# Expert layer on one core: the output product over all 16384 expert rows, and over a list of used rows

## The chip, the cores and the metric

The kernel runs on one core of a Trainium2 chip. TensorE (PE) multiplies, VectorE (DVE) and ScalarE (ACT) work on SBUF and PSUM, GpSimd (POOL) works on SBUF and issues DMAs, SyncE (SP) only issues DMAs. PEld is TensorE's weight load. The metric is device time in microseconds, the median of several executions.

## The reference, cut to what matters

Two layers, 256 tokens of 1024 numbers, float32. Each layer ends in an expert mixer:

```
def peer_ffn(h, w_query, sub_keys, expert_u, expert_v):   # 256 tokens
    scores = (h @ w_query) . sub_keys          # 8 heads, 2 halves, 128 keys
    s_top, i_top = top_k(scores, 16)           # in both halves
    best, pos = top_k(all 16*16 sums, 16)      # 16 experts for each head
    expert_idx = i_top_half0 * 128 + i_top_half1   # of the chosen pairs
    gates = softmax(best)
    a = gelu(expert_u[expert_idx] . h) * gates     # 128 per token
    return sum over the 128 of a * expert_v[expert_idx]
```

There are 128 x 128 = 16384 experts, and a token uses 128 of them. The layer before the mixer is retention (layer 0) or a spatial gating unit (layer 1). The change touches neither.

## The kernel before, in words

The expert mixer is computed densely. An expert has the number i*128 + j. For each i there is a tile of 128 rows (the j's, on the partitions), and 128 such tiles in a layer.

- **Every weight tile** (128x1024 float32, 512 KB) comes in through `split_load`: SP loads `raw`, ACT rounds it to `hi` (L140), DVE forms the rest `lo` (L141). Products are three matmuls, hi by hi, hi by lo and lo by hi. `raw`, `hi` and `lo` have three buffers, and `weight` keeps two tiles ahead of the one in use.
- **First product**: `u_pair` multiplies two tiles of `peer_u` with the tokens and puts the gelu into A (tiles 0 to 71, kept in SBUF) or into `at`, which POOL writes to `a_dram` (the 56 tiles 72 to 127, L843).
- **Routing** (`route`, `gates`): top-16 on DVE, beside the first 36 pairs of the first product.
- **Gates**: during the last 28 pairs, `gather` builds for four tokens at a time one-hot matrices and multiplies them on PE (L820). The result is the gate of all 16384 experts for these tokens, nearly all of it zero. DVE multiplies tiles 0 to 71 of A with it in place (L824), ACT copies the other 56 to G (L826).
- **Output product**: for each of the 128 tiles, `gated` takes the product of A and G (from A, or reloaded from `a_dram`, L859, and multiplied on POOL, L871), ACT and DVE split it (L874, L875), and `out_proj` multiplies it with the tile of `peer_v`: two token blocks of 128, three matmuls, two halves of 512 columns, 12 matmuls of 512 columns in all (L347). The sums of all tiles stay in four PSUM banks. `adag` is woven in, one step for a pair: SP loads a tile of `ada_w`, DVE multiplies and adds it (L246). In layer 0 it has 32 such tiles, in layer 1 eight.

The program is written in the order in which the code runs. A planner keeps the order on each engine, by a simulated time line, and each engine takes its instructions in that order; a wait of the first holds those behind it. SP's and POOL's DMAs are such instructions too.

## Time and profile before

| | |
|---|---|
| median of 3 runs | 2140.42 us (2136.84 to 2141.46) |
| span of the profiled execution | 2136.0 us |
| DMA over the span | 455.50 MB, mean 213 GB/s |
| product of layer 0, layer 1 (first to last L347 of it) | 713 to 1060 us, 1775 to 2123 us |

The profiled execution's own time lies among the three runs, so 0.8 to 5.5 us above its span. Times in rows are microseconds from the start of the span, unless marked ns. A busy share is an average over stages with different limits, so the rows below are taken stage by stage.

### The profile page before, as it was taken

How to read it: one execution, taken by the hardware profiler on the slowest of the kernel's cores; microseconds unless marked ns; L12 is line 12 of the kernel's file. 1: busy time of each engine (PE TensorE's matmuls, PEld its weight loads, DVE VectorE, ACT ScalarE, POOL GpSimd, SP SyncE). 2: the span in 40 equal slices, each digit the busy share in tenths (PEclk: the TensorE clock that was granted, in tenths of full speed). 3: DMA queues.
4: the chain of work that ended last, by engine and by line, in shares of the span. 5: the costliest groups of instructions: out<-in, count | busy, mean ns of one | idle time of the engine just before them, and what ended most of it. 6: DMA issues, size and time to landing. Idle time of an engine off the chain costs nothing.

```text
span 2136.0 us, 35285 instructions
## 1 busy us (share of the span) xinstructions
PE 2067.6 (97%) x13440; PEld 1872.9 (88%) x13440; DVE 1642.5 (77%) x2908; ACT 1102.0 (52%) x1648; POOL 272.3 (13%) x286
## 2 busy tenths in 40 slices
PE   4999899999999999999999998999999999999998
PEld 4988799999999888888787787999999998888886
DVE  7877678998988677765677786789889886655565
ACT  2444444446777544444454534444467774444443
POOL 1000001100000100033202700011000001000332
PEclk8999999999999999999999999999999999999999
DMA  7678455555555788877656775555555557656774
GB/s 270 214 250 272 155 180 181 180 184 184 180 192 188 265 274 275 276 256 244 225 184 210 243 245 187 171 187 179 186 179 188 184 197 270 230 191 209 241 240 161
DMA packets 127497, 455.50 MB, mean 213 GB/s; under 512 B 15328, under 2 KB 17392, under 8 KB 126816
## 3 DMA queue, kind: packets, MB, share of 16 engines
q1 hardware_dynamic: 115056, 411.36, 57.7%
q0 software_dynamic: 11984, 39.79, 5.8%
q8 instruction: 105, 1.72, 0.3%
q10 hardware_dynamic: 288, 2.10, 0.3%
q14 instruction: 64, 0.52, 0.1%
HBM read 435.36 MB, written 17.83 MB: 212 GB/s over the span
## 4 chain that ended last, share of the span: by engine, by line
PE 92%; DVE 3%; DMA 1%; issue 1%; ACT 1%; POOL 1%; SPq 0%; DVEq 0%; ACTq 0%; POOLq 0%
PE acc L347 36%; PE ps L173 17%; PE ps L174 17%; PE ps L175 17%; PE gps L820 3%; DVE lo L141 1%; PE ps L667 1%; PE ps L292 1%; DMA x<-in_x 0%; PE ps L254 0%; DVE ada L246 0%; ACT hi L140 0%; POOL vr L591 0%; DMA raw<-in_sgu_out 0%; ACT ht L307 0%
## 5 line engine op out<-in xcount | busy, mean ns | idle before, releaser
L140 ACT CAST hi<-raw 128x1024 fp32r<-128x1024 f32 x680 | 713.6, 1050 | 788.1 <-PE ps L174 380.8
L141 DVE TENSOR_TENSOR lo<-raw,hi 128x1024 fp32r<-128x1024 f32 x680 | 855.7, 1259 | 290.4 <-ACT hi L140 288.3
L173 PE MATMUL ps<-hh,hi 128*128 128x256 f32 x2432 | 699.4, 288 | 7.1 <-ACT hh L312 7.1
L174 PE MATMUL ps<-hl,hi 128*128 128x256 f32 x2432 | 691.9, 285 | 0.8 <-DVE hl L313 0.7
L175 PE MATMUL ps<-hh,lo 128*128 128x256 f32 x2432 | 690.6, 284 | 1.1 <-DVE lo L141 1.1
L173 PEld LDWEIGHTS ps<-hh,hi 128*128 128x128 f32 x2432 | 468.7, 193 | 8.3 <-ACT hh L312 8.3
L174 PEld LDWEIGHTS ps<-hl,hi 128*128 128x128 f32 x2432 | 469.3, 193 | 1.4 <-DVE hl L313 1.4
L175 PEld LDWEIGHTS ps<-hh,lo 128*128 128x128 f32 x2432 | 468.5, 193 | 1.4 <-DVE lo L141 1.4
L347 PE MATMUL acc<-lo,wh 128*128 128x512 f32 x1008 | 311.6, 390 | 0.0
L347 PE MATMUL acc<-hi,wl 128*128 128x512 f32 x1008 | 310.5, 389 | 0.0
L347 PE MATMUL acc<-hi,wh 128*128 128x512 f32 x1008 | 271.5, 389 | 0.0
L347 PEld LDWEIGHTS acc<-hi,wl 128*128 128x128 f32 x1008 | 189.3, 188 | 39.4
L347 PEld LDWEIGHTS acc<-hi,wh 128*128 128x128 f32 x1008 | 189.1, 188 | 39.2
L347 PEld LDWEIGHTS acc<-lo,wh 128*128 128x128 f32 x1008 | 188.3, 188 | 38.4
L174 PE MATMUL ps<-lo,hh 128*128 128x512 f32 x320 | 126.3, 395 | 3.4 <-DVE lo L141 3.4
L175 PE MATMUL ps<-hi,hl 128*128 128x512 f32 x320 | 125.9, 394 | 0.0
L246 DVE SCALAR_TENSOR_TENSOR ada<-adaw,c_act,ada 128x1024 f32<-128x1024 f32 x84 | 107.7, 1283 | 19.2 <-PE acc L347 13.6
L711 POOL TENSOR_TENSOR eq<-eq,tif 128x512 f32<-128x512 f32 x32 | 56.6, 1785 | 454.4 <-DVE eq L706 405.9
L173 PE MATMUL ps<-hi,hh 128*128 128x512 f32 x320 | 112.8, 392 | 0.0
L871 POOL TENSOR_TENSOR at<-at,G 128x512 f32<-128x512 f32 x56 | 83.8, 1497 | 192.9 <-DMA at<-a_dram 192.8
L815 DVE TENSOR_TENSOR og<-oo,half 128x512 f16<-128x512 f16 x256 | 96.0, 417 | 0.1
L805 ACT ACTIVATE oo<-iota_f,jT 128x128 f16<-128x128 f32 x256 | 84.7, 431 | 5.3 <-PE gps L820 3.0
(215 smaller groups left out, 2000.2 us busy)
## 6 DMA issues: line engine op xcount, KB each, us to landing
raw<-in_peer_u SPq DMA_DIRECT2D x256, 512.0 KB, 3.5
raw<-in_peer_v SPq DMA_DIRECT2D x256, 512.0 KB, 4.3
adaw<-in_ada_w SPq DMA_DIRECT2D x96, 512.0 KB, 4.7
raw<-in_sgu_in SPq DMA_DIRECT2D x48, 512.0 KB, 4.4
raw<-in_ret_vg SPq DMA_DIRECT2D x32, 512.0 KB, 4.2
raw<-in_peer_q SPq DMA_DIRECT2D x32, 512.0 KB, 3.6
a_dram<-at POOLq DMA_DIRECT2D x56, 256.0 KB, 2.8
at<-a_dram POOLq DMA_DIRECT2D x56, 256.0 KB, 4.0
```

The source lines that it names most:

```text
L140: after_mark(nc.scalar.copy(hi, raw), after[0], ORDER)
L141: after_mark(nc.vector.tensor_tensor(lo, raw, f(hi), op=ALU.subtract), after[1], ORDER)
L173: first = nc.tensor.matmul(ps, ah, bh, start=start, stop=False)
L174: nc.tensor.matmul(ps, ah, bl, start=False, stop=False)
L175: marks["pe"] = nc.tensor.matmul(ps, al, bh, start=False, stop=stop)
L246: op = nc.vector.scalar_tensor_tensor(a, w, c_act[:, dc:dc + 1], a, op0=ALU.mult, op1=ALU.add)
L347: marks["pe"] = nc.tensor.matmul(accs[b][n], a[:, tb], bb[:, n * 512:(n + 1) * 512], start=first and a is lh and bb is wh, stop=False)
L711: nc.gpsimd.tensor_tensor(eq, eq, tif[:, :, a, :].unsqueeze(2).to_broadcast([P, NTB, TOPK, TOPK]), op=ALU.mult)
L805: nc.scalar.activation(oj[:, k // 2, :, k % 2], iota_f, AF.Abs, bias=jT[:, t0 + k:t0 + k + 1], scale=-1.0)
L815: nc.vector.tensor_tensor(og[:, q], oi[:, q].unsqueeze(1).to_broadcast([P, 2, P, 2]), gH[:, :, t:t + 2].unsqueeze(2).to_broadcast([P, 2, P ...
L820: nc.tensor.matmul(ps[:, 2 * q + k, :], oj[:, q, :, k], og[:, q, e, :, k], start=e == 0, stop=e == 1)
L871: nc.gpsimd.tensor_tensor(w, w, G[:, ip * 2 - n0:ip * 2 - n0 + 2, :], op=ALU.mult)
```

## The change

- A keeps only tiles 0 to 31 (`N0`). The first products of the other 96 (`NG`) are written by POOL to a table in DRAM, in two DMAs for a pair. The table has one line of 2 KB for each expert: activation and gate of token block 0, activation and gate of block 1, 128 tokens each.
- G is now one buffer for each token block. When a block is full, four times (24 tiles each) DVE takes the maximum over the 128 tokens (`flags`) and ACT issues a DMA that writes the gates to the table.
- `sort_rows` makes lists of used rows: those with a gate in block 0 alone, in both, and in block 1 alone. Room is for 23, 38 and 23 columns of 128 rows (`CAP`). Places come from prefix sums, the lists from one-hot products on PE (96 matmuls of 168 columns into one PSUM tile). A branch (`tc.If`) handles rows for which there is no room.
- The output product begins with 12 pairs (`FIRST`) of tiles 0 to 23 as before, while the lists are made (two steps for a pair, in the first ten). Then 19 units of two "both" columns, 23 units of one column of each "alone" list, and the four pairs left of A are interleaved. For each listed column POOL issues two indirect DMAs: 128 lines of the table (2 KB of a line, or 1 KB) and 128 rows of `peer_v` (4 KB each). An "alone" column has one token block, so 6 matmuls instead of 12.

```diff
-N0 = 72
+N0 = 32
+NR = 72
+NG = P - N0
-N1 = 128
+CAP = (23, 38, 23)
+NC = sum(CAP)
+FIRST = 12
 def split_load
+        if index is not None:
+            raw = listed["pool"].tile([P, 1024], F32, tag="vraw", bufs=5, name=nm("vraw"))
+            row_gather(raw, I["peer_v"], index)
+        else: ... nc.sync.dma_start(raw, src)
+    def row_gather(dst, table, index):
+        nc.gpsimd.indirect_dma_start(
+            out=dst, out_offset=None, in_=table,
+            in_offset=bass.IndirectOffsetOnAxis(ap=index, axis=0))
 def u_rows
+            for b in range(NTB):
+                nc.gpsimd.dma_start(cells[:, i1:i1 + 2, b, 0, :], tmp[:, :, b * P:(b + 1) * P])
 def gather
-                nc.scalar.copy(G[:, :, t0:t0 + 4], pi[:, n0:, :])
+            nc.scalar.copy(G[b][:, :, tt:tt + 4], pi[:, n0:, :])
+            if tt == P - 4:
+                for c in range(0, NG, 24):
+                    nc.vector.tensor_reduce(flags[:, b, c:c + 24], G[b][:, c:c + 24, :],
+                                            axis=AX.X, op=ALU.max)
+                    nc.scalar.dma_start(cells[:, 1 + c:25 + c, b, 1, :], G[b][:, c:c + 24, :])
 def lists
+            for i in range(0, NG, 8):
+                pm = pool.tile([P, 4, P, 2], F16, tag="pm", bufs=2, name=nm("pm"))
+                nc.vector.tensor_tensor(pm, iota_h..., pairs(ih[:, 0, i:i + 8], P), op=ALU.is_equal)
+                nc.vector.tensor_tensor(eq, cols_h..., pairs(ih[:, 1, i:i + 8], ncol), op=ALU.is_equal)
+                nc.vector.tensor_tensor(cm[:, :, 0], eq, pairs(rows_h[:, i:i + 8], ncol), op=ALU.mult)
+                nc.scalar.mul(cm[:, :, 1], eq, pidx)
+                for k in range(8):
+                    nc.tensor.matmul(ps, pm[:, k // 2, :, k % 2], cm[:, k // 2, :, :, k % 2], ...)
+                yield
 output product
+        def fetch(unit):
+            cell = vp.tile([P, 2, wide], F32, tag="cell" + kind, name=nm("cell"))   # 3 buffers
+            for a in range(2):
+                row_gather(cell[:, a], ag if kind == "b" else halves, listed["ag"][:, cs[a]:cs[a] + 1])
+        def gated(unit):
+            if kind == "b":
+                for b in range(NTB):
+                    nc.gpsimd.tensor_tensor(w[:, :, b * P:(b + 1) * P], cell..., cell..., op=ALU.mult)
+                return split_unit(w, T)
+            nc.gpsimd.tensor_tensor(w, cell[:, :, :P], cell[:, :, P:], op=ALU.mult)
+        for pos, unit in enumerate(order):
+            if pos < FIRST - 2: two steps of sorter
+            if last:
+                with tc.If(nc.values_load(listed["count"][:1, :1], min_val=0, max_val=NG * P) > 0):
+                    leftovers(*spare)
+            if pos + 2 < len(order):
+                fetch(order[pos + 2])
+            nxt = gated(order[pos + 1])
+            if kind == "x": half_proj(a, ...)      # 6 matmuls for a column
+            else: out_proj(accs, ...)              # 12 matmuls
```

## Rows read from the trace of the kernel before

**Rows 1.** Chain of waits in time order, the products: start, us, engine, tile, line, count.

```profile
713.01 60.33 PE acc L347 x266
...
949.78 110.66 PE acc L347 x488
...
1759.86 0.94 PE gps L820 x16
1775.23 60.32 PE acc L347 x266
...
1862.43 257.55 PE acc L347 x1136
```

**Rows 2.** Busy by stretch: us, engine busy (count), PEclk, DMA share, GB/s.

```profile
6.00:31.00 25.00, 6.10 (x40) 5.94 (x40) 21.00 (x33) 4.52 (x10) 2.13 (x2) 0.95 0.99 393
...
498.00:713.00 215.00, 215.00 (x2033) 212.59 (x2032) 182.26 (x368) 154.77 (x324) 19.68 (x31) 1.00 0.56 189
713.00:780.00 67.00, 67.00 (x302) 55.54 (x301) 48.05 (x50) 32.65 (x38) 5.36 (x5) 1.00 0.82 281
780.00:1060.00 280.00, 280.00 (x1252) 232.02 (x1251) 191.54 (x193) 134.20 (x154) 52.82 (x52) 1.00 0.79 260
...
1840.00:2123.00 283.00, 283.00 (x1254) 234.18 (x1253) 167.03 (x162) 135.21 (x155) 51.04 (x51) 1.00 0.65 212
```

**Rows 3.** Groups by line, DVE: name, shapes, count, busy us, mean ns, idle before.

```profile
L141 DVE TENSOR_TENSOR lo<-raw,hi 128x1024 fp32r<-128x1024 f32 x680 | 855.7, 1259 | 290.4 <-ACT hi L140 288.3
...
L246 DVE SCALAR_TENSOR_TENSOR ada<-adaw,c_act,ada 128x1024 f32<-128x1024 f32 x84 | 107.7, 1283 | 19.2 <-PE acc L347 13.6 <-PE ps L175 2.5 <-DMA adaw<-in_ada_w 2.4
L815 DVE TENSOR_TENSOR og<-oo,half 128x512 f16<-128x512 f16 x256 | 96.0, 417 | 0.1
...
L875 DVE TENSOR_TENSOR wl<-at,wh 128x512 fp32r<-128x512 f32 x56 | 40.4, 721 | 31.2 <-ACT wh L874 31.0
...
L715 DVE TENSOR_REDUCE sel<-eq 128x32 f32<-128x512 f32 x32 | 21.5, 671 | 2.6 <-POOL eq L711 2.4
...
L703 DVE CAST pf<-pa 128x64 f32<-128x64 uint32 x16 | 3.1, 194 | 0.5
```

**Rows 4.** Groups by line, POOL, costliest first.

```profile
L871 POOL TENSOR_TENSOR at<-at,G 128x512 f32<-128x512 f32 x56 | 83.8, 1497 | 192.9 <-DMA at<-a_dram 192.8
...
L859 POOL DMA_DIRECT2D at<-a_dram x56 | 32.4, 578 | 193.1 <-DVE wl L875 185.8 <-DMA a_dram<-at 7.3
L843 POOL DMA_DIRECT2D a_dram<-at x56 | 30.4, 543 | 386.8 <-ACT at L754 247.7 <-ACT G L826 129.8 <-ACT hi L140 9.3
```

**Rows 5.** Time line of POOL alone: one small read and multiply, start and us.

```profile
247.42 0.55 POOL L218 TENSOR_TENSOR rs<-v,mhalf 128x1 f32<-128x1 f32 x1 [1.30 <-DVE v L234]
```

**Rows 6.** Time line of DVE, gates and then tail of the first product.

```profile
600.60 0.75 DVE L815 TENSOR_TENSOR og<-oo,half 128x512 f16<-128x512 f16 x2
...
708.25 1.23 DVE L141 TENSOR_TENSOR lo<-raw,hi 128x1024 fp32r<-128x1024 f32 x1 [1.61 <-ACT hi L140]
711.12 1.23 DVE L141 TENSOR_TENSOR lo<-raw,hi 128x1024 fp32r<-128x1024 f32 x1 [1.65 <-ACT hi L140]
```

**Rows 7.** DMA issues: queue, count, KB each, median us from issue to landing.

```profile
raw<-in_peer_v SPq DMA_DIRECT2D x256, 512.0 KB, 4.3
...
a_dram<-at POOLq DMA_DIRECT2D x56, 256.0 KB, 2.8
at<-a_dram POOLq DMA_DIRECT2D x56, 256.0 KB, 4.0
```

**Rows 8.** Issue instructions of one line on SP: ns min/median/max.

```profile
L137 SPq DMA_DIRECT2D raw<-in_peer_v x256: 327/328/328, 700.2 to 2111.6; - x128
```

**Rows 9.** POOL's multiply L871 by itself: ns min/median/max.

```profile
L871 POOL TENSOR_TENSOR at<-at,G x56: 1273/1460/2324, 715.3 to 2105.7; 128x512 f32<-128x512 f32 x56
```

**Rows 10.** Time line of all engines, around one multiply on POOL.

```profile
726.00 1.22 DVE L141 TENSOR_TENSOR lo<-raw,hi 128x1024 fp32r<-128x1024 f32 x1
...
726.74 1.63 POOL L871 TENSOR_TENSOR at<-at,G 128x512 f32<-128x512 f32 x1 [3.88 <-DMA at<-a_dram]
...
727.76 1.69 DVE L141 TENSOR_TENSOR lo<-raw,hi 128x1024 fp32r<-128x1024 f32 x1 [0.55 <-ACT hi L140]
```

More of the change, by code (lines that the diff above doesn't have):

```diff
@@ L63, in peer_v_order, with unit_weights @@
 def peer_v_order():
-    n0, n1 = N0 // 2, N1 // 2
-    return list(range(n0)) + list(range(n0, n1)) + list(range(n1, P // 2))
+    nat = [("n", ip) for ip in range(N0 // 2)]
+    both = [("b", c) for c in range(CAP[1] // 2)]
+    one = [("x", c) for c in range(CAP[0])]
+    rest, last = nat[FIRST:], both.pop()
+    mixed = []
+    n = max(len(both), len(one))
+    for k in range(n):
+        for group in (both, one, rest):
+            mixed += group[len(group) * k // n:len(group) * (k + 1) // n]
+    return nat[:FIRST] + mixed + [last]
+def unit_weights(layer, kind, c):
+    if kind == "n":
+        return [("peer_v", layer, c * 2 + a) for a in range(2)]
+    if kind == "b":
+        return [("peer_g", layer, BASE[1] + c * 2 + a) for a in range(2)]
+    return [("peer_g", layer, BASE[0] + c), ("peer_g", layer, BASE[2] + c)]
 def weight_order():
@@ L94, in weight_order @@
             yield "peer_q", layer, m
-        for i in range(N1):
+        for i in range(P):
             yield "peer_u", layer, i
-        for ip in peer_v_order():
-            if ip * 2 >= N1:
-                for a in range(2):
-                    yield "peer_u", layer, ip * 2 + a
-            for a in range(2):
-                yield "peer_v", layer, ip * 2 + a
+        for unit in peer_v_order():
+            yield from unit_weights(layer, *unit)
 @with_exitstack
@@ L155, in weight @@
                 break
+            if k[0] == "peer_g":
+                ready.append((k, split_load(None, listed["v"][:, k[2]:k[2] + 1])))
+                continue
             src = I[k[0]]
-            for j in k[1:]:
-                src = src[j]
+            if k[0] == "peer_v":
+                src = src[bass.ds((k[1] * P + k[2]) * P, P)]
+            else:
+                for j in k[1:]:
+                    src = src[j]
             ready.append((k, split_load(src)))
@@ L765, in peer @@
         emitted = 0
-        slots = PH - 2 + n0 // 2
+        slots = PH - 2 + NR // 2
         q = None
-        for k in range(PH + n0 // 2):
+        for k in range(PH + NR // 2):
             marks["gate"] = marks["pe"]
@@ L773, in peer @@
             else:
[L774 to L775 removed]
+                u_rows(k - PH)
                 q = None
@@ new lines, in sort_rows @@
+        def sort_rows():
+            nc.vector.tensor_scalar(flags, flags, 0.0, None, op0=ALU.is_gt)
+            masks = lp.tile([P, 3, NG], F32, name=nm("masks"))
+            nc.vector.tensor_tensor(masks[:, 1], flags[:, 0], flags[:, 1], op=ALU.mult)
+            nc.vector.tensor_tensor(masks[:, 0], flags[:, 0], masks[:, 1], op=ALU.subtract)
+            nc.vector.tensor_tensor(masks[:, 2], flags[:, 1], masks[:, 1], op=ALU.subtract)
+            yield
+            place, left = numbers(masks, CAP, BASE, lp, ps_tile())
+            yield
+            for got in lists(place, NC, lp, ps_tile()):
+                yield
+            row, listed["v"] = got
+            agi = lp.tile([P, NC], I32, name=nm("agi"))
+            one, two, three = (slice(BASE[c], BASE[c] + CAP[c]) for c in range(3))
+            nc.vector.tensor_scalar(agi[:, one], row[:, one], 2.0, None, op0=ALU.mult)
+            nc.vector.tensor_copy(agi[:, two], row[:, two])
+            nc.vector.tensor_scalar(agi[:, three], row[:, three], 2.0, 1.0,
+                                    op0=ALU.mult, op1=ALU.add)
+            listed["ag"] = agi
+            yield
+            listed["left"] = left
+            count = lp.tile([P, 1], F32, name=nm("count"))
+            nc.vector.tensor_reduce(count, left, axis=AX.X, op=ALU.add)
+            ch = lp.tile([P, 1], F16, name=nm("ch"))
+            nc.vector.tensor_copy(ch, count)
+            ps = ps_tile()
+            nc.tensor.matmul(ps[:1, :2], ch, ones_h, start=True, stop=True)
+            ci = lp.tile([1, 2], I32, name=nm("ci"))
+            nc.vector.tensor_copy(ci, ps[:1, :2])
+            listed["count"] = ci
+            yield
@@ L880, in peer @@
+        sorter = sort_rows()
         nxt = gated(order[0])
-        for pos, ip in enumerate(order):
+        nstep = -(-18 // (FIRST - 2))
+        for pos, unit in enumerate(order):
             wh, wl = nxt
+            kind, c = unit
+            if pos < FIRST - 2:
+                for _ in range(nstep):
+                    next(sorter, None)
+            if pos == FIRST - 3:
+                drain(sorter)
+            last = pos == len(order) - 1
+            if last:
+                spare = ps_tile(), ps_tile()
+                with tc.If(nc.values_load(listed["count"][:1, :1], min_val=0, max_val=NG * P) > 0):
+                    leftovers(*spare)
```

210 lines of the change are left out of this document (168 added, 42 removed).

## The prediction

> **What bounds the kernel now.** I read the chain of waits first, in time order. In both products it is TensorE alone: layer 1 has one piece of 1136 matmuls in 257.55 us without a wait, 0.2267 us for one of 512 columns, and the pieces of layer 0 give the same [rows 1]. The table by stretch says the same: in the output product PE is busy all the time, DVE for 68% in layer 0 (191.54 of 280), POOL for 19%. In the last part of the first product (498 to 713) PE is also always busy, with DVE at 85% [rows 2]. So a matmul that goes is time that goes, as long as nothing else becomes the slowest. What could: DMA moves 260 GB/s there at a busy share of 0.79, while the start of the kernel, where loads alone set the pace, shows 393 GB/s at 0.99 [rows 2].
>
> **The change part by part, for one layer.**
>
> *Matmuls that go.* After the change there are 32 full tiles, 38 full columns and 46 half ones: 93 tiles' worth instead of 128. 35 x 12 x 0.2267 = **-95.2 us**. This holds only if the room suffices. I ran the reference's routing on its inputs: the lists hold 2599, 4753 and 2771 rows in layer 0, and 2665, 4383 and 2508 in layer 1, where 2944, 4864 and 2944 fit. So the branch is not taken.
>
> *Matmuls that come.* The lists take 96 of 168 columns. 16 gate matmuls of 128 columns take 0.94 us, 0.059 each [rows 1]; between that and 0.2267 for 512 columns, 168 columns come to 0.076: **+7.3** (5.7 to 21.8, by the two rows).
>
> *Used rows, block 0, amid the first product.* Four maxima of 3072 elements on DVE. One of 512 takes 0.671, and 512 more elements cost DVE 0.538 (1.259 for 1024 against 0.721 for 512, both split operations) [rows 3]: 3.36 each, 13.4 together, in one lump. DVE's 32.7 idle us of that stretch [rows 2] are spread, and a lump is covered only by the two tiles that are split ahead, 3.8 us each (215 us for 56 tiles): **+6** (0 to 13.4). ACT's four DMAs lie beside it if an issue is as short as SP's, 0.33 us [rows 8]. These have 3072 pieces of 512 bytes; if ACT were held until its 1.57 MB had gone, it would be 4.0 us each at 393 GB/s, 8.3 at 189, so 16 to 33 for a block. I take the short one, as the only HWDGE issue that the rows show; the long one stays in the range.
>
> *Used rows of block 1 and the lists, around the first ten pairs.* DVE has the second lump of 13.4. A list step compares and multiplies 1024 + 672 + 672 float16 numbers; two operations of 512 end 0.75 after the start, the second 0.335 later than the first (0.417 for one alone) [rows 3, 6], so 1.55 a step and 18.6 for twelve. About 38 small operations of at most 288 elements, at 0.25 each (0.194 for 64 elements [rows 3]), make 9.5. Together 41.5. Room: ten pairs last 54.4 us, and DVE is idle for 18.95 of 67 there [rows 2], 15.4; two further pairs 3.1; the last four tiles of the first product 1.6 each [rows 6], 6.5; two tiles ahead 5.4. 41.5 - 30.4 = **+11** (0 to 28). DVE's instructions are in order: behind the lists wait `lo` and `wl`, and for these PE.
>
> *POOL, the step that decides.* From the 13th unit on, each of 84 columns needs two indirect DMAs, and they sit in one queue with the multiplies. 168 issues; 61 multiplies of 256 elements (two for each of 19 units, one for each of 23) at half of 1.497 [rows 4], 0.75, make 45.8. The matmuls of this stretch (19 + 4 full units, 23 half) are 828 x 0.2267 = 187.7 us. No row shows an indirect DMA. From below, a direct one with 128 lines holds POOL for 0.54 to 0.58 [rows 4]. From above I take the multiply, which reads two whole operands on 128 partitions: 1.497 [rows 4]. An indirect one has to write as many descriptors and first to read one number from each partition, which is what the smallest POOL operation does, 0.55 [rows 5]. The two added give 1.1, my value; it lies in the middle of the bounds. Then POOL needs 168 x 1.1 + 45.8 = 230.6. It can begin about 10 us before PE gets there (two units in `vraw` and cells). 230.6 - 187.7 - 10 = **+33** (0 at 0.9 or less; +100 at 1.5). Landing is no limit: 4.0 us [rows 7], while a unit's four issues and its multiply last longer than that.
>
> *Transfers of that stretch.* 92 tiles of `peer_v` 48.2 MB, cells 16.0 MB, and in layer 0 23 tiles of `ada_w`, 12.1 MB: 76.3 and 64.2. Dividing rate by busy share gives 329 and 326 GB/s full in the two products, 397 at the start [rows 2]. So layer 0 needs 192 to 232 us and layer 1 162 to 197. Layer 1 is hidden behind POOL's 221. In layer 0 I take 228: **+7**, in layer 0 only.
>
> *The branch.* Every engine reads a count and jumps before the last unit. Nothing in the trace shows one. The bounds are 0 and three landings of 4.3 in a row [rows 7], 12.9 (the count, the code, the start again); I take **+5**, near one landing. None of these costs goes below nothing, since PE was never idle.
>
> *Costs nothing.* 96 writes of activations by POOL instead of 28 (0.54 each [rows 4]) are hidden by POOL's idle time: 19.7 busy of 215 [rows 2]. Reloads and multiplies of 28 pairs leave POOL; nobody waited for them, as PE shows no gap.
>
> **Sum.** Layer 1: -95.2 + 7.3 + 6 + 11 + 33 + 5 = -32.9. Layer 0: -25.9. Together -58.8. The profiled execution: 2136.0 - 58.8 = 2077 of span, and with the 4.4 by which the median of the runs stands above this span (its own time lies 0.8 to 5.5 above) **2082 us**.
>
> **A rule weighed.** POOL's multiply takes 1.273 at least, 1.497 on average and 2.324 at most [rows 4, 9], and a split on DVE that overlaps one takes 1.69 instead of 1.22 [rows 10]. The Trainium skill, "SBUF — State Buffer", section "Who interferes with whom", says that a DVE instruction with two SBUF inputs and a GpSimd instruction that reads SBUF hold each other off, the second waiting for the whole of the first. The trace agrees for the multiply. Whether it goes for the reading of an index list no row shows. By the rule it would, and by the multiply's mean delay (1.497 - 1.273 = 0.22) an issue would be 1.32, POOL +37 more in each layer, layer 0's transfers hidden behind it, and the sum 2149.
>
> **The rivals.**
>
> *A. An indirect issue costs as little as a direct one.* At 0.58 POOL needs 143 us and hides. PE sets the pace in layer 1; in layer 0 the transfers, 192 us at the best rate seen, +5. For: 128 descriptors in both. Against: the index list. Sum: -95.2 + 29.3 = -65.9 and -60.9, time **2014**. The Trainium skill, "DMA: Bandwidth & Descriptors", section "Specifications", gives about 358 GB/s as HBM's limit for a core; by it layer 0 would lose 20 us more. The 393 GB/s of rows 2 are above that.
>
> *B. Slower: POOL's queue holds PE up for longer than the matmuls saved.* The costs other than POOL's are 29.3 (layer 1), so the change loses once POOL costs 66, and that is 168 x t + 45.8 - 197.7 = 66: from **t = 1.29 us** for an issue. For: the queue is in order, so a wait for a free `vraw` or a cell adds to t; +0.22, as the multiply has it on average over its least [rows 4, 9], is enough; 128 numbers from as many partitions may be read one by one. Against: the bare sum of its two parts is 1.1. At 1.5 POOL costs 100, so +34 in each layer, the transfers of layer 0 being hidden: **2209**. ACT held by the gates' DMAs would add to this, but does not decide it.
>
> *C. Transfers decide, not POOL.* At 326 to 329 GB/s, +35 in layer 0 and 0 in layer 1 (197 against 197.7): with POOL at 0.9, **2043**. For: 4 KB rows in any order, and cells of 1 and 2 KB. Against: 397 at the start.
>
> *D. It doesn't do what it says.* If room ran out, the branch's 96 columns of 12 matmuls would add at least 261 us. The counts speak against it.
>
> **How the numbers follow.** Forecast (issue 1.0 to 1.25) 0.40, A 0.24, B 0.26, C 0.08, D 0.02. An issue of 0.1 us more is 34 us in all (less in layer 0 while the transfers hide it), so the forecast's own range is 2045 to 2130. The range has to reach well into A and B: **1995 to 2190**, which leaves out A at its luckiest (no lump, no branch cost) and B beyond t = 1.44. No change within 0.2% (4.3 us, about what a measurement of this kernel can tell) is the narrow strip about t = 1.29: 0.04, taken from the top of the forecast and the bottom of B. Faster 0.71, slower 0.25.
>
> **What would show it.** Groups by line: the mean of the indirect DMA on POOL, 1.1; under 0.9 is A, over 1.29 is B. By stretch: after the 12th pair, POOL busy over 95% and PE about 85%, with a stretch of some 220 us instead of 283 for the same tiles; if it is the DMA share that is at 0.95 or more and POOL has gaps, it is C. DVE without a gap from 700 to 770, and PE waiting for `lo` there for some 11 us. A gap in PE of 6 us where the first block of gates ends; a longer one with ACT idle means that ACT was held by its DMAs. What makes the prediction wrong is above all the issue time, and then anything that stops POOL's queue.

## The result, and the profile after

The changed kernel takes **2285.78 us** (median of 4 runs, 2283.4 to 2286.64) where the kernel before, run beside it, takes 2139.3: 1.0685 of it, interval 1.067 to 1.07. Forecast were 2082 us, range 1995 to 2190. The change makes the kernel 146 us slower; the sign was wrong, and the time lies beyond the range. The span is 2284.1 us, 148.1 more than before.

The head of the page (busy time, share, instructions; then the granted clock in 40 slices):

```profile
PE 2006.8 (88%) x12796; PEld 1757.7 (77%) x12796; DVE 1683.7 (74%) x3041; ACT 1091.9 (48%) x1636; POOL 791.5 (35%) x771
...
PEclk8999999999999988888999999999998989888998
```

The same line of the kernel before:

```profile
PE 2067.6 (97%) x13440; PEld 1872.9 (88%) x13440; DVE 1642.5 (77%) x2908; ACT 1102.0 (52%) x1648; POOL 272.3 (13%) x286
```

PE is busy 60.8 us less than before and yet the span grew: it now waits where it did not. The table by stretch of layer 0 shows where; the columns are those of [rows 2] (stretch, length, busy time of PE, PEld, DVE, ACT and POOL, then granted clock, DMA share, GB/s), whose second to fourth rows cover the same work.

```profile
498.00:611.50 113.50, 113.50 (x1068) 112.25 (x1067) 93.10 (x203) 87.33 (x176) 28.50 (x36) 1.00 0.64 197
611.50:636.00 24.50, 10.37 (x86) 9.69 (x85) 20.72 (x20) 7.01 (x13) 2.89 (x4) 0.72 0.99 281
636.00:712.00 76.00, 76.00 (x721) 75.05 (x720) 61.22 (x143) 58.65 (x123) 14.45 (x20) 0.98 0.64 198
712.00:746.50 34.50, 23.10 (x185) 22.12 (x183) 24.79 (x26) 8.72 (x13) 4.33 (x6) 0.85 0.94 282
746.50:821.00 74.50, 74.38 (x391) 59.70 (x390) 67.54 (x113) 40.26 (x47) 7.69 (x9) 1.00 0.80 264
821.00:839.00 18.00, 0.40 (x2) 0.00 (x0) 3.48 (x4) 2.40 (x3) 14.33 (x15) 0.57 0.75 254
839.00:1128.50 289.50, 231.58 (x835) 167.25 (x836) 173.40 (x172) 112.19 (x136) 242.28 (x211) 0.89 0.74 245
```

Three places lose. Behind each block of gates PE stands (rows two and four: 25.5 us idle, and the clock falls to 0.72 and 0.85). In front of the first half column it stands 18 us (row six). In the stretch of the listed columns (last row) it is busy for 80%, at a granted clock of 0.89, and POOL is the full engine, not PE: busy for 242 of 289.5 us, and nearly all the rest is the short gaps of the next rows.

POOL's groups (columns as in [rows 4]):

```profile
L168 POOL DMA_INDIRECT vraw<-in_peer_v,vi x168 | 201.1, 1197 | 110.8 <-DVE agi L1004 69.2 <-issue 32.9 <-DMA vraw<-in_peer_v,vi 3.0
L168 POOL DMA_INDIRECT cell<-ag_dram,agi x168 | 197.1, 1173 | 48.5 <-issue 41.1 <-DMA vraw<-in_peer_v,vi 3.4 <-POOL at L1062 1.9
...
L1057 POOL TENSOR_TENSOR at<-cell 128x256 f32<-128x256 f32 x76 | 74.7, 1008 | 0.6
...
L1062 POOL TENSOR_TENSOR at<-cell 128x256 f32<-128x256 f32 x46 | 49.6, 1079 | 0.7
```

An indirect DMA holds POOL for 1.185 us on average. Beside that the idle column shows 74.0 us of "issue" in the two groups: 0.30 us stand ahead of nearly each one. From POOL's first gather (812.9) to the end of its last (1121.5) its time line has no gap over 0.31 us: the queue is 308.6 us of work and these gaps, and 306.5 in layer 1. The time line of POOL where the queue starts shows both (start, us, and in brackets the idle time):

```profile
834.46 0.95 POOL L168 DMA_INDIRECT cell<-ag_dram,agi  x1 [0.30 <-issue]
835.72 0.94 POOL L168 DMA_INDIRECT vraw<-in_peer_v,vi  x1 [0.30 <-issue]
836.96 0.94 POOL L168 DMA_INDIRECT vraw<-in_peer_v,vi  x1 [0.30 <-issue]
837.92 0.74 POOL L1062 TENSOR_TENSOR at<-cell 128x256 f32<-128x256 f32 x1
```

The gap stands ahead of an indirect DMA and not ahead of a multiply, which starts 0.02 after the one before it. And the first multiply stands behind nineteen gathers, though the first cells were issued at 815.8 and land 4.6 us after their issue at the median; PE waits for that multiply and ACT's split of it, by its own time line:

```profile
839.15 1.22 PE L1069 MATMUL acc<-hi,wh 128*128 128x512 f32 x2 [17.75 <-ACT wh L1045]
```

**The account of both layers**, from PE's time line (ends of its pieces). A layer's output product ends with its last pair of tiles, whose 24 matmuls stand on other lines than the rest; 1060 and 2123 us, in the table of the kernel before, leave them out. The last matmuls of both layers, before and then changed:

```profile
1065.47 0.39 PE L175 MATMUL acc<-hi,wl 128*128 128x512 f32 x1
2125.03 0.39 PE L175 MATMUL acc<-hi,wl 128*128 128x512 f32 x1
```

```profile
1137.20 0.39 PE L209 MATMUL acc<-hi,wl 128*128 128x512 f32 x1
2272.80 0.39 PE L209 MATMUL acc<-hi,wl 128*128 128x512 f32 x1
```

Layer 0: first product +33.7 (746.7 against 713.0), first twelve pairs +9.4 (74.7 against 24 x 12 x 0.2267 = 65.3), gap +17.8, stretch from the first half column to the end 298.4 against 287.6 for the same tiles, +10.8: in all +71.7. Layer 1, from the end of layer 0's output product: +34.6, +8.6, +20.0 and +12.8 (297.7 against 284.9), in all +76.0. What follows it is 0.4 longer. The sum is the 148.1.

### The profile page after: what moved, and what is told of

The parts are those of the page before. It is cut to its first block, busy times and chain, and to the rows that moved or that the text cites. A ratio compares the mean times of both kernels' runs of the same rounds, so it can differ in the third digit from the quotient of the medians.

```text
span 2284.1 us, 34636 instructions
## 1 busy us (share of the span) xinstructions
PE 2006.8 (88%) x12796; PEld 1757.7 (77%) x12796; DVE 1683.7 (74%) x3041; ACT 1091.9 (48%) x1636; POOL 791.5 (35%) x771
## 5 line engine op out<-in xcount | busy, mean ns | idle before, releaser
L162 ACT CAST hi<-raw 128x1024 fp32r<-128x1024 f32 x488 | 509.7, 1048 | 582.1 <-PE ps L208 349.9
L163 DVE TENSOR_TENSOR lo<-raw,hi 128x1024 fp32r<-128x1024 f32 x488 | 616.1, 1266 | 126.6 <-ACT hi L162 120.7
L163 DVE TENSOR_TENSOR lo<-vraw,hi 128x1024 fp32r<-128x1024 f32 x168 | 222.1, 1327 | 231.9 <-ACT hi L162 225.7
L817 POOL DMA_DIRECT2D ag_dram<-at x192 | 139.0, 726 | 527.9 <-ACT at L807 519.2
L162 ACT CAST hi<-vraw 128x1024 fp32r<-128x1024 f32 x168 | 175.4, 1047 | 278.8 <-DMA vraw<-in_peer_v,vi 235.3
L168 POOL DMA_INDIRECT vraw<-in_peer_v,vi x168 | 201.1, 1197 | 110.8 <-DVE agi L1004 69.2
L168 POOL DMA_INDIRECT cell<-ag_dram,agi x168 | 197.1, 1173 | 48.5 <-issue 41.1
L397 PE MATMUL acc<-lo,wh 128*128 128x512 f32 x544 | 183.0, 419 | 2.5 <-DVE lo L163 1.5
L397 PE MATMUL acc<-hi,wl 128*128 128x512 f32 x544 | 175.4, 405 | 0.0
L397 PEld LDWEIGHTS acc<-lo,wh 128*128 128x128 f32 x544 | 106.0, 201 | 34.8 <-DVE lo L163 13.4
```

The lines of the kernel that those rows point to most:

```text
L162: after_mark(nc.scalar.copy(hi, raw), after[0], ORDER)
L163: after_mark(nc.vector.tensor_tensor(lo, raw, f(hi), op=ALU.subtract), after[1], ORDER)
L168: nc.gpsimd.indirect_dma_start(out=dst, out_offset=None, in_=table, in_offset=bass.IndirectOffsetOnAxis(ap=index, axis=0))
L397: marks["pe"] = nc.tensor.matmul(accs[b][n], a[:, tb], bb[:, n * 512:(n + 1) * 512], start=first and a is lh and bb is wh, stop=False)
L817: nc.gpsimd.dma_start(cells[:, i1:i1 + 2, b, 0, :], tmp[:, :, b * P:(b + 1) * P])
```

## The experiments

The stretch and the end of the first product are read from PE's time line in each kernel. For layer 1 the first product is counted from the end of layer 0's output product. The kernels e2, e3 and e4 fetch other rows than the listed ones; e5, e13 and e15 leave the gates out of the listed tiles, e6 and e15 miss used rows, and e8 leaves a rest out; the sizes and the number of matmuls stay.

| kernel | first product ends, layer 0 | first product, layer 1 | stretch, layer 0 / 1 | us | ratio to before |
|---|---|---|---|---|---|
| before | 713.0 | 709.4 | 287.6 / 284.9 for the same tiles | 2139.3 | 1 |
| changed | 746.7 | 744.0 | 298.4 / 297.7 | 2285.78 | 1.067 to 1.07 |
| e2_v_direct | 744.9 | 744.5 | 223.4 / 197.7 | 2085.7 | 0.970 to 0.980 |
| e3_cells_direct | 747.9 | 744.3 | 222.7 / 202.0 | 2093.92 | 0.974 to 0.984 |
| e4_both_direct | 747.9 | 740.8 | 217.1 / 189.4 | 2073.74 | 0.966 to 0.974 |
| e8_no_lo | 746.9 | 744.8 | 262.9 / 254.5 | 2205.18 | 1.028 to 1.034 |
| e7_in_order | 746.0 | 743.7 | 321.3 / 318.0 | 2299.6 | 1.072 to 1.078 |
| e1_gates_by_pool | 739.4 | 740.6 | 306.5 / 293.4 | 2293.93 | 1.065 to 1.080 |
| e5_long_pieces | 736.4 | 729.4 | 301.9 / 293.8 | 2255.61 | 1.051 to 1.058 |
| e6_short_maxima | 751.6 | 747.6 | 299.9 / 292.5 | 2272.94 | 1.060 to 1.066 |
| e9_spread | 754.0 | 745.8 | 299.5 / 294.2 | 2298.81 | 1.073 to 1.077 |
| e13_no_gate_writes | 736.2 | 734.1 | 303.6 / 293.0 | 2264.09 | 1.056 to 1.060 |
| e15_no_writes_short | 716.2 | 712.4 | 304.7 / 296.1 | 2222.87 | 1.034 to 1.041 |
| e10_80_listed | 740.7 | 738.7 | 269.6 / 258.8 | 2184.87 | 1.019 to 1.023 |
| e11_80_listed_dve | 742.3 | 735.8 | 255.8 / 234.3 | 2133.7 | 0.995 to 0.999 |
| e12_72_listed_dve | 739.0 | 731.7 | 267.0 / 248.4 | 2148.37 | 1.003 to 1.006 |
| e14_80_listed_paced | 735.9 | 724.5 | 239.5 / 218.0 | 2128.77 | 0.994 to 0.998 |

The theory after the result was that POOL's queue alone sets the end of the output product, and that the hold in the first product is ACT standing behind its own gate DMAs. The rivals were transfers, DVE, and the order of POOL's queue.

### Is it POOL's queue? Indirect DMAs replaced by direct ones

**e2_v_direct**: SP loads tiles of `peer_v` in order in place of the listed rows.

```diff
-            row_gather(raw, I["peer_v"], index)
+            nc.sync.dma_start(raw, I["peer_v"][bass.ds(tile * P, P)])
...
```

> The 84 listed columns of a layer take a contiguous tile of peer_v by SP's direct load (the wrong rows, the same bytes) into the same five buffers; the cells are still gathered. Theory (POOL's queue sets the pace: 168 issues of 1.48 us with the gap behind them, and multiplies of 62 us, 311 in all): 84 issues remain, POOL needs about 186 us, the stretch from the first half column falls from 289 to 195 to 215 us, and the time to 2070 to 2130. Rival (transfers set the pace: the bytes are the same): the stretch stays above 270 us, time above 2240. Rival (the planner's order on POOL, multiplies late behind gathers, sets it): the 18 us gap before the first half column stays and the time is 2180 to 2240.

**e3_cells_direct**: the cells instead, from lines of the table in order.

```diff
-                row_gather(cell[:, a], ag if kind == "b" else halves,
-                           listed["ag"][:, cs[a]:cs[a] + 1])
+                nc.sync.dma_start(cell[:, a], ag[bass.ds((1 + cs[a]) * P, P), :wide])
```

> The cells of the 84 listed columns come by SP's direct load from contiguous lines of the table (the wrong lines, the same bytes); peer_v's rows are still gathered by POOL. Theory (issues on POOL count, whatever they fetch): the same 84 issues fewer, so within 30 us of the run in which the rows of peer_v come direct, 2070 to 2130. Rival (rows of 4 KB in any order are what is slow, or the wait for cells): the time differs from that run by more than 60 us.

**e4_both_direct**: both edits.

> Both the cells and the rows of peer_v of the listed columns come by SP's direct loads (wrong rows, same bytes); POOL only multiplies. Theory (POOL's queue): POOL has 62 us of work and drops out; what is left is PE's 188 us or the transfers, 76 MB in layer 0 in 192 to 232 us; stretch 190 to 235 in layer 0 and 188 to 200 in layer 1, time 2050 to 2110. If the transfers were the bound all along, nothing is gained here either: above 2240.

Either half of the indirect DMAs taken away, with the same bytes and the same matmuls, turns the change into a gain: 2085.7 and 2093.92. 84 indirect DMAs fewer in a layer shorten the stretch by 75 to 100 us; 84 x 1.485 (1.185 and the 0.30 ahead) would be 125. The 84 that are left take longer, 1.317 and 1.346 on average, and PE is busy for 92% of layer 0's stretch in both, so that its own work is nearly the limit. Without any, layer 1's stretch is 189.4, PE's own 187.7; layer 0's is 217.1, and there the transfers are full, as this stretch of it shows:

```profile
839.00:1020.00 181.00, 167.41 (x719) 131.22 (x718) 160.02 (x155) 97.08 (x119) 68.90 (x54) 0.99 0.98 359
```

The DMA engines are full at 359 GB/s, and 217.1 is inside the prediction's 192 to 232 us for that traffic. DVE is busy for 160 of the 181 us too, and PE's waits name its `lo` for 11.0 of 15.3 us, so that the transfers alone hold layer 0 is argued, not shown. The Trainium skill, "DMA: Bandwidth & Descriptors", section "Specifications", names about 358 GB/s as HBM's limit for a core; this row agrees, the 393 of [rows 2] does not. The theory stands. The whole saving of the matmuls exists in layer 1 (284.9 to 189.4 for the same tiles) and 70 us of it in layer 0, and POOL's queue takes it and more.

### What makes an indirect DMA 1.19 us? The index read beside DVE

In layer 0, 54 of the 168 indirect DMAs have no DVE instruction beside them for over 0.3 us; their mean is 0.952. The 114 others have 1.32 (worked out from the time lines of POOL and DVE, 805 to 1125). **e8_no_lo** takes the larger of the two-input DVE instructions of the listed columns away (the correction term uses `hi` a second time; `wl` stays).

```diff
-        lo = spool.tile([P, 1024], F32R, tag="lo", name=nm("lo"))
+        lo = hi if index is not None else spool.tile([P, 1024], F32R, tag="lo", name=nm("lo"))
         after_mark(nc.scalar.copy(hi, raw), after[0], ORDER)
+        if index is not None:
+            return hi, lo
```

> For listed columns DVE doesn't form lo; the products take hi in its place (one split left out, matmuls the same). Theory (an indirect DMA waits on POOL for DVE operations with two SBUF operands: 1.32 us where they overlap, 0.96 where not): the mean issue falls from 1.185 to 1.0 to 1.08, multiplies from 1.0 to about 0.8, POOL saves 30 to 45 us a layer, time 2195 to 2235. Rival (contention is not what makes the long ones): the mean stays above 1.15 and the time above 2265.

2205.18, inside the theory's numbers. POOL's groups in it:

```profile
L170 POOL DMA_INDIRECT cell<-ag_dram,agi x168 | 171.8, 1023 | 49.7 <-issue 44.4 <-DMA cell<-ag_dram,agi 2.1 <-DMA vraw<-in_peer_v,vi 1.8
L170 POOL DMA_INDIRECT vraw<-in_peer_v,vi x168 | 167.6, 998 | 105.9 <-DVE agi L1006 65.6 <-issue 29.0 <-ACT hi L162 4.1
...
L1059 POOL TENSOR_TENSOR at<-cell 128x256 f32<-128x256 f32 x76 | 61.2, 831 | 0.8 <-DVE wl L1048 0.2
...
L1064 POOL TENSOR_TENSOR at<-cell 128x256 f32<-128x256 f32 x46 | 37.0, 804 | 0.8
```

No instruction of POOL was touched, and each became shorter: 1.185 to 1.01, the multiplies 1.03 to 0.82. The gap of 0.30 stayed. So DVE's operations with two SBUF inputs lengthen an indirect DMA as they lengthen a multiply. That it is the two inputs, and not DVE's being busy, the time lines of all runs bear out, in a few cases: 41 indirect DMAs that had only DVE's `adas` or `dg` beside them, with one such input at most, took 0.96 on average, 1068 with no DVE instruction beside them 0.95, and those beside one with two inputs 1.28 (six beside a wider instruction with one input, `ada<-adaw,c_act`, took 1.08). This is the rule that the prediction weighed and did not take (the Trainium skill, "SBUF — State Buffer", "Who interferes with whom"); it does go for the indirect DMA here.

### Does POOL's order matter?

**e7_in_order** ties POOL's gathers and multiplies into the order in which they are written, so that no multiply stands behind later gathers.

```diff
+    def in_order(inst):
+        after_mark(inst, listed.get("last"), ORDER)
+        listed["last"] = inst
+        return inst
...
-            row_gather(raw, I["peer_v"], index)
+            in_order(row_gather(raw, I["peer_v"], index))
...
```

> POOL's gathers and multiplies in the output product are kept in the order in which the program writes them, instead of the planner's, which puts 20 gathers ahead of the first multiply. Theory (POOL's total sets the end): the 18 us gap before the first half column shrinks, but the stretch behind it grows by as much; time 2270 to 2295. Rival (the order costs time by itself): 30 to 40 us less, 2240 to 2260.

The gap in front of the first half column falls from 17.8 to 4.2 us, the stretch grows from 298.4 to 321.3, and the whole gets 14 us slower, 5 us above the theory's numbers; the rival is out. Removing the gap wins nothing, since POOL's queue comes out no shorter: 318.4 us instead of 308.6 in layer 0. In order, POOL's multiplies also wait for their cells (9.7 us there).

### The first product: who holds PE?

The waits of PE in the changed kernel up to 760 name ACT alone (us in total, times, longest):

```profile
PE ps L207 <- ACT hi L162: 23.9, 3, 10.7
PE acc L397 <- ACT hi L162: 1.6, 1, 1.6
```

and ACT's time line shows it at its own DMA issues (`ACTq` is its queue):

```profile
611.51 16.62 ACTq L893 DMA_DIRECT2D ag_dram<-G x4
628.26 0.60 ACT L807 ACTIVATE at<-ps 128x512 f32<-128x512 f32 x1 [16.25 <-issue]
```

while DVE has its four maxima in the same stretch:

```profile
612.90 13.12 DVE L891 TENSOR_REDUCE flags<-G 128x24 f32<-128x3072 f32 x4
```

**e1_gates_by_pool** lets POOL issue the gate DMAs.

```diff
-                    nc.scalar.dma_start(cells[:, 1 + c:25 + c, b, 1, :], G[b][:, c:c + 24, :])
+                    nc.gpsimd.dma_start(cells[:, 1 + c:25 + c, b, 1, :], G[b][:, c:c + 24, :])
```

> Only change to the changed kernel: the sixteen DMAs that write the gates to the table are issued by POOL instead of ACT. Theory (ACT is held by its own DMA issue, 4 of them 16.6 us, twice a layer): ACT's wait in front of the gelu, 62.7 us in all, goes; PE's waits for hi at the two blocks (10.7 and 9.8 in layer 0) shrink to a few us that DVE's four maxima leave; time about 2225 us (2210 to 2240). Rival 1 (DVE's lump of 13.4 us makes the stall): ACT is free, but PE now waits for lo as long as before, time 2270 to 2286. Rival 2 (the table writes fill the DMA engines, share 0.99 there, and the weight tiles come late): PE waits for hi behind a late raw, time 2265 to 2286.

A miss: POOL issues each in 1.42 us, ACT is no longer held by an issue, and the first product ends only 7.3 us earlier; the first twelve pairs then lose 11.5. The time is 2293.93, no gain. PE's waits up to 760 already name DVE:

```profile
PE ps L209 <- DVE lo L163: 7.1, 2, 6.0
PE gps L882 <- DVE og L877: 5.9, 1, 5.9
```

**e5_long_pieces** writes the same gate bytes in runs of 12 KB to a buffer of their own (the table's gate half takes a second copy of the activations, so the product uses these in place of the gates).

```diff
-                nc.gpsimd.dma_start(cells[:, i1:i1 + 2, b, 0, :], tmp[:, :, b * P:(b + 1) * P])
+                for g in range(2):
+                    nc.gpsimd.dma_start(cells[:, i1:i1 + 2, b, g, :], tmp[:, :, b * P:(b + 1) * P])
...
-                    nc.scalar.dma_start(cells[:, 1 + c:25 + c, b, 1, :], G[b][:, c:c + 24, :])
+                    nc.scalar.dma_start(g_dram[layer][:, b, c:c + 24, :], G[b][:, c:c + 24, :])
```

> The gates of a block go, still in four DMAs on ACT with the same bytes, to a buffer of their own in pieces of 12 KB instead of 512 bytes; the table's gates take a second copy of the activations, written pair by pair (so gates are left out of the result). Theory (3072 short pieces hold ACT and crowd the DMA engines): the issue falls from 16.6 us for four to under 2, the first product ends 12 to 25 us earlier in layer 0 and stays ahead, time 2225 to 2265. Rival (DVE's lump of 13.4 us alone makes the stall at each block): the first product ends within 5 us of before, time 2275 to 2295.

In the stretch of the lump the DMA engines move 373 GB/s instead of 281 at the same share, and PE is idle 8.1 of 24.5 us instead of 14.1:

```profile
611.50:636.00 24.50, 16.44 (x126) 15.55 (x125) 22.48 (x26) 7.87 (x15) 5.78 (x8) 0.79 0.98 373
```

Four issues take 3.0 us instead of 16.62. So pieces of 512 bytes matter; but two thirds of the first product's loss in layer 0 stayed (23.4 of 33.7). The time came as the theory had it, the first product's gain in layer 0 did not (10.3, and 12 at least was expected).

**e6_short_maxima** lets DVE's maxima run over 8 of 128 tokens.

```diff
-                    nc.vector.tensor_reduce(flags[:, b, c:c + 24], G[b][:, c:c + 24, :],
+                    nc.vector.tensor_reduce(flags[:, b, c:c + 24], G[b][:, c:c + 24, :8],
```

> The maxima look at 8 of the 128 tokens of a block only (lists miss rows; every list, gather and product keeps its size). DVE's lump falls from 13.4 us to about 1.4. Theory (writes are the cause, the lump is hidden beside them): the first product ends within 8 us of the changed kernel's 746.7, and the time is 2262 to 2290, a little less by what the lump costs ahead of the lists. Rival (the lump is the cause): it ends 20 us earlier or more, time under 2250.

The first product ends later (751.6), not earlier. I read this as acquitting DVE, and that was wrong: e1's waits name it, and two later runs show it.

**e9_spread** cuts each block's writes and maxima into twelve, one a step.

```diff
-                for c in range(0, NG, 24):
...
+                pending.extend((b, c) for c in range(0, NG, 8))
...
             step[0] += 1
+            spill_gates(1)
```

> The gate writes and the maxima of a block are cut into twelve pieces of 8 tiles (twelve issues of 1024 short rows in place of four of 3072), one in each step of the first product, so that ACT and DVE never stand in one lump; block 0's twelve lie in the steps that remain, block 1's mostly still come together at its end. Lists, gathers and the output product are as in the changed kernel. Theory (the first product's +33.5 us a layer come from the lump: ACT held by its own issue, PE's buffers not drained): the first product of layer 0 ends between 722 and 737 instead of 746.7, the time is 2240 to 2268. Rival (the short rows cost the DMA engines the same wherever they are issued): the first product ends at 743 to 750, the time is 2276 to 2296.

It did not test what it meant to: the planner put the twelve issues of block 0 together again, and ACT stood there for 24 us:

```profile
610.00 0.37 ACTq L899 DMA_DIRECT2D ag_dram<-G  x1
...
610.88 1.57 ACTq L899 DMA_DIRECT2D ag_dram<-G  x2
...
612.48 8.42 ACTq L899 DMA_DIRECT2D ag_dram<-G  x3
...
621.01 13.47 ACTq L899 DMA_DIRECT2D ag_dram<-G  x6
```

The first issues take 0.4 us, the later ones 2.2 to 2.8 on average: an issue by itself is short, and it holds ACT when others stand shortly before it. The end of the first product (754.0) and the time lie above both forecasts.

**e13_no_gate_writes** is e5 without any gate write.

```diff
-                    nc.scalar.dma_start(cells[:, 1 + c:25 + c, b, 1, :], G[b][:, c:c + 24, :])
+                    pass
```

> The gates of the listed tiles are not written to device memory at all (the table's gate half takes a second copy of the activations, as in the kernel with long pieces, so the lists and the gathers stay and the output differs from the reference); maxima, lists, gathers and multiplies stay. Theory (PE's waits of 14.1 and 9.8 us behind ACT's casts and the lowered clock after them are all due to the gate writes): the first product of layer 0 ends at 712 to 722 instead of 746.7, the whole time falls by 45 to 75 us to 2210 to 2240. Rival (the maxima and the gate copies of DVE and ACT, or the second traffic of the activations, hold PE as well): it ends at 730 to 742, about as with long pieces (736.4), and the time is 2245 to 2265.

The theory missed, the rival's numbers came (736.2; the time of 2264.09 is at their upper end): without ACT's issues PE waits 14.6 us instead of 25.5, and its waits name DVE for 13.0 of them, which has its 13.13 us of maxima at the same place:

```profile
PE ps L209 <- DVE lo L163: 7.1, 2, 6.0
PE gps L883 <- DVE og L878: 5.9, 1, 5.9
...
612.73 13.13 DVE L892 TENSOR_REDUCE flags<-G 128x24 f32<-128x3072 f32 x4
```

**e15_no_writes_short** takes both away (e13's edit and e6's).

> As the kernel without gate writes, and its maxima run over 8 of 128 tokens (the flags, and so the lists, come from those tokens alone; what is computed differs from the reference further). Without the writes the first product of layer 0 still ended at 736.2, with PE idle 7.0 of 20 us behind DVE (lo and og) while DVE runs its four maxima in one lump of 13.1 us; with short maxima but the writes it ended at 751.6, behind ACT. Theory, formed from those two: the two lumps begin at the same moment and cover each other, so that either alone holds PE for its 13 to 17 us, and only without both the hold goes: the first product of layer 0 ends at 712 to 722, the time falls to 2195 to 2240. Rival (a third thing holds PE: the copies of the gate tiles by ACT, the doubled activations' traffic): it ends at 730 to 738 as without the writes alone, and the time is 2250 to 2270.

Now PE never waits in the first product, and the clock stays full:

```profile
600.00:640.00 40.00, 40.00 (x384) 39.53 (x384) 35.61 (x88) 30.79 (x66) 17.36 (x24) 1.00 0.74 222
640.00:700.00 60.00, 60.00 (x582) 59.27 (x581) 49.51 (x111) 47.47 (x100) 23.97 (x34) 1.00 0.77 228
700.00:745.00 45.00, 45.00 (x292) 39.58 (x292) 35.39 (x65) 24.93 (x31) 10.76 (x15) 1.00 0.80 262
```

It ends at 716.2 (713.0 before), and layer 1's takes 712.4 (709.4 before): of 33.7 and 34.6 us, 3 are left. Two lumps on two engines began within 1.4 us of each other, 16.6 us of ACT and 13.1 of DVE, and covered each other. Each alone holds PE, so each taken away alone looked like no cause or a third of one.

### A version that beats both

List fewer tiles, until POOL's queue fits PE's stretch. **e10_80_listed** keeps 48 tiles whole (e9's spread is in it):

```diff
-N0 = 32
+N0 = 48
-CAP = (23, 38, 23)
+CAP = (19, 32, 19)
...
-            raw = listed["pool"].tile([P, 1024], F32, tag="vraw", bufs=5, name=nm("vraw"))
+            raw = listed["pool"].tile([P, 1024], F32, tag="vraw", bufs=4, name=nm("vraw"))
...
```

> 80 of 128 tiles are listed instead of 96 (48 stay whole; 70 list columns instead of 84: 140 indirect DMAs and 51 multiplies an output product instead of 168 and 61), the gate writes spread as in the kernel with spread gates, one raw buffer of peer_v fewer. Theory (POOL's queue sets the end of the output product at 1.48 us an indirect DMA and 1.0 a multiply: 311 us of queue, here 258): the stretch from the first half column to the end of the output product shrinks from 298 by 45 to 60 us, to 238 to 253, although PE has some 16 us more of matmuls in it; time 2130 to 2175. Rival (the stretch goes by PE, its clock or the bytes transferred, which grow or stay): stretch 285 to 315, time 2250 to 2310.

The stretch fell by 29 and 39 us, less than the 45 to 60 that the theory gave, though PE has 16 us more to do in it; the time is 10 us over the theory's numbers. The direction is the theory's and the rival is out; the size is not met. POOL's groups show why:

```profile
L168 POOL DMA_INDIRECT cell<-ag_dram,agi x140 | 178.2, 1273 | 40.9 <-issue 36.0 <-POOL at L1070 3.2 <-DMA vraw<-in_peer_v,vi 0.9
L168 POOL DMA_INDIRECT vraw<-in_peer_v,vi x140 | 173.1, 1237 | 148.5 <-DVE agi L1012 107.9 <-issue 30.4 <-DVE lo L163 7.1
```

An indirect DMA is longer here, 1.255 on average for 1.185, with DVE beside more of them (110 of 140 in layer 0). So POOL's queue lasts 275.8 and 268.6 us instead of the 258 expected, 33 and 38 less than in the changed kernel, and the stretch fell by nearly the same.

**e11_80_listed_dve** takes the multiplies from POOL too:

```diff
-                    nc.gpsimd.tensor_tensor(w[:, :, b * P:(b + 1) * P],
+                    nc.vector.tensor_tensor(w[:, :, b * P:(b + 1) * P],
...
```

> As the kernel with 80 listed tiles, and the gate multiplies of the listed columns are made by DVE instead of POOL, which then holds indirect DMAs alone: 140 x 1.48 = 207 us, just under the 215 us that PE needs for the stretch (187.7 in the kernel without indirect DMAs, 16 more whole tiles at 2.72 less 6 whole and 8 half list columns). Theory: the stretch falls to 212 to 235 us, and the 18 us gap in front of the first half column goes, since no multiply stands behind gathers any more: time 2050 to 2110, below both kernels. Rival (DVE becomes the bound, or its added reads of two SBUF inputs hold POOL's index reads as long as the multiplies did): the stretch stays at 240 to 260 and the time at 2125 to 2180, no better than with POOL's multiplies.

2133.7, ratio 0.9972 (0.9954 to 0.9991): 152 us under the changed kernel and just under the one before. The gap in front of the stretch is gone (0.5 us) as expected, and the rest of the stretch goes by PE, busy for 203 of 220 us:

```profile
815.00:850.00 35.00, 23.39 (x80) 16.21 (x79) 22.35 (x31) 11.25 (x14) 28.02 (x23) 0.80 0.84 275
850.00:1070.00 220.00, 202.87 (x849) 155.22 (x848) 165.62 (x208) 107.61 (x128) 139.81 (x111) 0.99 0.83 291
```

But in its first 35 us PE still waits a third of the time, and the stretch of 255.8 and 234.3 is, in layer 0, in the rival's 240 to 260 and, in layer 1, at the end of the theory's 212 to 235, the time 24 us above the theory's 2110 and inside the rival's 2125 to 2180. An indirect DMA still takes 1.217. The busy PE and the lost gap speak for the theory's mechanism; its size is not met, and the rival's part in that is not separated. By the expectation's own terms PE needs 204 us for the stretch, not 215, so the gap to it is wider still.

**e12_72_listed_dve** lists 72 (`N0 = 56`, `CAP = (17, 30, 17)`).

> As the kernel before it, but 72 of 128 tiles are listed (64 list columns: 128 indirect DMAs, 189 us of POOL; PE's stretch some 11 us longer, 226 us). Theory: if POOL no longer sets the end with 80 listed, the fewer listed tiles only cost matmuls here, and the stretch is PE's, 225 to 240 us: time 2065 to 2125, up to 25 us over the kernel with 80. Rival (POOL's queue still sets the end there): this kernel is 15 to 40 us faster than the one with 80 listed.

15 us slower than with 80, as the theory had the order; the rival, POOL still setting the end, had it faster, and POOL's gathers of `peer_v` here wait 127.2 us for DVE's `lo`, that is for a free buffer (52.4 in e11). The edit also takes `vraw` from four buffers to three and `pm` from two to one, so how much of the 15 us is matmuls isn't shown. The time itself is above the 2125 named.

**e14_80_listed_paced** is e11 with every gate piece tied behind the newest matmul:

```diff
-                nc.scalar.dma_start(cells[:, 1 + c:8 + 1 + c, b, 1, :], G[b][:, c:c + 8, :])
+                after_mark(nc.scalar.dma_start(
+                    cells[:, 1 + c:8 + 1 + c, b, 1, :], G[b][:, c:c + 8, :]), marks["pe"])
...
-            spill_gates(1)
+            if step[0] % 3 == 0:
+                spill_gates(1)
```

> The kernel with 80 listed tiles and DVE's multiplies, but each of the twelve gate pieces of a block is tied behind the newest matmul of its step, one in every third step, so that block 0's are issued over some 70 us of the first product; block 1's stay together at its end. Theory (it is the lump that holds ACT and fills the DMA engines): block 0's 14 us of PE idle time around 611 to 636 fall below 5, the first product of layer 0 ends 8 to 16 us earlier than the 742.3 of the kernel without the tie (726 to 735), and the time is 2100 to 2125. Rival (the writes take the same from the DMA engines wherever they stand, and ACT waits for each): the first product ends at 739 to 746 and the time is 2125 to 2145.

With 80 listed tiles a block has ten pieces. Those of block 0, spread from 615 to 718, take 0.37 to 0.39 us each, and the first product ends 6.4 us earlier than in e11, just short of the theory's numbers; the pieces of block 1 now hold up the first twelve pairs (95.2 us instead of 73.0), and the stretch is 16 us shorter. 2128.77, which is the rival's time, ratio 0.9959 (0.9942 to 0.9976), is 5 us under e11, with overlapping runs. Both are faster than the kernel before by 0.3 to 0.4%, and that is all that I got out of it.

## Why the prediction was wrong

**The step that failed is "POOL, the step that decides".** It took 1.1 us for an indirect issue; in the queue it costs 1.185 busy and 0.30 ahead of it, 1.485. The multiplies, taken at 0.75, half of [rows 4], take 1.008 and 1.079. The step's own formula with these gives 168 x 1.485 + 63.1 - 197.7 = +115 where it had +33; the trace shows 298.4 - 187.7 = +111 in layer 0, the branch in it. Two errors made the size. First, 1.1 was the sum of a direct issue and the smallest POOL operation, and for the busy time that was near (0.952 with no DVE beside it), but it priced neither the gap between two issues nor DVE's presence. Second, the rule on DVE's two inputs was written down, priced at 1.32 an issue, and set aside because no row showed it for an index. Beside DVE it measured 1.32; that the figures are alike is luck, since the rule's 1.32 was 1.1 and 0.22 for every issue, and measured were 0.952 and 0.37 on it beside DVE, 1.185 over all. The rule alone would not have saved the forecast: by it the sum was 2149, barely on the right side of the kernel before and 137 us short of the result.

**Rival B was what happened**, with its place, price and break-even point: t is over 1.29, and the change loses. At t = 1.5 it gave 2209. What lies between that and 2286 is the first product and the gap:

- *The lump of block 0, +6, with block 1's in the +11*: the maxima came as priced, 13.12 us for four against 13.4. ACT's issue was taken at SP's 0.33 us [rows 8]; it measured 4.57 at the median and 8.02 at most, 16.62 for the four of one block. The prediction had worked out 16 to 33 as the long end, and chose the short one as "the only HWDGE issue that the rows show", a row of 128 pieces for a DMA of 3072. The first product lost 33.7 and 34.6 instead of 6 (e15 shows that both lumps together are all of it but 3 us).
- *The gap of 18 and 20 us* in front of the first half column has no step in the prediction. It counted POOL's head start as 10 us gained; the planner spent the head start on gathers and put the multiply that PE waits for behind them. e7 shows that it is no loss by itself: in the written order the queue is no shorter.
- *Lists and first ten pairs, +11 and +7.3*: 9.4 and 8.6 measured for twelve pairs. That is the list matmuls, put at 7.3, and hardly more; DVE's overrun, the +11, did not show: PE is busy for 74.38 of 74.50 us there.
- *PE's clock* has no term: every matmul was priced at full clock, as [rows 2] have it, and behind stalls it was lower (last section).

**Right were** the matmuls gone (without indirect DMAs layer 1's stretch is 189.4, 187.7 worked out), the room of the lists, the transfers of layer 0 (217 within 192 to 232, with DVE nearly as full), and the branch in sign: PE waits 2.8 us for it in layer 0, 5 were taken.

**What stays open**: why the 0.30 us stand ahead of each indirect DMA (no run changed them), and why the stretches of e11 and e14 are longer than PE's own 204 us, by 52 and 30 us and by 36 and 14. A form with two index columns in one indirect DMA, which would have halved their number, wasn't tried.

## What to carry to other kernels

Before counting the matmuls that a sparse gather saves, count the gather's instructions on the queue that issues them, at the price they have next to that stretch's DVE work and with the gap between two of them, and choose the size of the sparse part so that this queue is shorter than what is left for TensorE. Price a DMA issue by the pieces that were issued shortly before it on its queue (here 0.37 us for the first of four, 3.6 to 8.0 for the others), and keep such issues off an engine that TensorE waits for. When two lumps start at the same time on two engines, take both away in one run before acquitting either.

## What the runs showed of the hardware that I had not expected

- An indirect DMA costs POOL the same for rows of 4 KB (`vraw`, median 0.978 us) and of 1 and 2 KB (cells, 0.953), 128 rows each, and 0.30 us stand ahead of the next one; behind a multiply it is 0.16.
- Four DMAs of 3072 pieces of 512 bytes hold ACT for 16.62 us, and in that stretch the DMA engines are full at 281 GB/s (share 0.99); with the same bytes in 12 KB runs they move 373 GB/s (0.98). Issues of 1024 such pieces, one every 10 us or more, take 0.37 to 0.39.
- A stall of PE costs more than its length: layer 0's first product lost 33.7 us, of which 25.5 are idle time and 2.1 four early matmuls of the output product. The granted clock was 0.72, 0.85 and 0.57 in the stretches with stalls, and 0.89 over the whole stretch of the listed columns, where PE had many short waits; it was 1.00 in all of these before [rows 2]. These are mixtures of its two levels, 1.2 and 2.4 GHz (0.5 and 1.0): from 611.5 to 618, with PE still busy, it was 1.00, from 618 to 628, with PE busy for 1.15 us, 0.71, and from 628 to 636 it was 0.50. Behind the gap in front of the first half column, two matmuls of 512 columns took 1.05 us at first (840.17) instead of 0.62.
